# Planned waits of layer 0's attention steps, and the transposes of P and of the convolution in one PSUM bank

## The chip, the cores and the metric

One core of a Trainium2 chip runs the whole program. TensorE (PE) multiplies matrices into PSUM, VectorE (DVE), ScalarE (ACT) and GpSimd (POOL) do elementwise work, and SyncE (SP), ACT and POOL start DMAs. Each engine takes its instructions in the order in which they stand in its own stream and waits on semaphores for the others. The metric is the device time of one execution in microseconds (us); lower is better.

## The reference

A decoder trunk of two layers over 512 tokens of width 1024, in float32. Only the mixer of layer 0 is touched here: attention over a window of 128 tokens (8 query heads, 2 key heads, a learned sink per head) beside a convolution module, with one input and one output projection.

```
def even_mixer(h, w_in, sinks, conv_w, conv_b, ln_g, ln_b, w_out, pos):
    proj = einsum('bsd,de->bse', h, w_in)
    q, k, v, glu = split(proj, [512, 640, 768])
    a = band_attention(rotary(q), rotary(k), v, 127, sinks)      # 8 heads of 64
    g_a, g_b = split(glu, 2)
    c = causal_depthwise_conv(g_a * sigmoid(g_b), conv_w, conv_b)  # 31 taps, 512 channels
    c = silu(layer_norm(c, ln_g, ln_b))
    return einsum('bse,ed->bsd', concatenate([a, c]), w_out)
# trunk: h += mixer(rms_norm(h)); h += swiglu(rms_norm(h)); twice; then rms_norm
```

## The kernel before, in words

Activations lie transposed: 128 features on the partitions, 512 tokens along the row. Every weight block of 128x128 is split into a high and a low part (`w_hi` by ScalarE, `w_lo` by VectorE or, in this mixer, by GpSimd), and a product is three matmuls of 512 columns, L201 to L203 in `acc3`, "a tile" below. A projection onto 128 outputs is 8 tiles, 24 matmuls.

Layer 0's mixer is one list of steps (`C0["steps"]`, L39): `g0` to `g3` are the two projections of a block of the gated unit and its convolution, `k`, `v` and `q0` to `q3` the projections of attention, `S0` to `S3` start the scores of two heads, `V0` to `V3` their product with V, `L` the norm behind the convolution. `A`, `X` and `Y` are tiles of the output projection that read attention's four results, `B` and `C` those that read the convolution's four.

The order of TensorE's stream is written by a small planner at build time, `Seq` (L208). It has a clock, `seq.t`, in estimated microseconds of TensorE work; each tile moves it on by a constant (L204, L265). Scores, values and norms are generators in lines of their own. Each yields a cost and a wait: the planner emits the next piece at the first tile at which the wait is over. So a wait is a number of tiles put between two pieces, and no instruction that waits. Where the next step needs a result, `seq.until` moves the clock on at once to the time of the next piece (L236): no tile is left to put in between. The other engines' streams are ordered by the scheduling layer, which plays the program through a timeline of its own.

The pieces that the change touches:

- `scores0(i)` (L573): waits `q`; 8 score matmuls for the first two blocks of 128 tokens, a wait `S`, 8 for the other two (L590, L591). VectorE takes mask and minimum out of banks 2 and 3 (L598), ScalarE the exponentials into `Pm` (L610), VectorE the sums and `rl` (L605, L614, L615). After a wait `ST` the values may follow.
- `values0(i)` and `pt_av` (L620, L395): P is transposed in four groups into a bank (L407), copied by ScalarE into `pts` (L410) and multiplied with V (L421). `TA` is planned between the transpose and its product, `AO` before the output step: VectorE scales by `rl` into `on` (L430), TensorE transposes `on` (L435), and two engines split it into `oh` and `ol`. Transposes take banks 4 and 7 in turn.
- `conv_tile(j)` (L467): 31 taps of the convolution of 128 channels, the first ones on ScalarE and GpSimd (L478, L479), the others on VectorE, one instruction a tap, accumulating in bank 6 (L481, L483), and a sum into `yc` (L484). They have the lowest priority, so that the scheduling layer puts them between the rest.
- `conv_norm` (L633): for each of the four blocks, not before `ln[j]` on the planner's clock, four transposes of `yc` into bank 7 (L641), statistics (L643), and a copy into `yn` (L644). After the fourth: mean and variance (L650, L652), a power on GpSimd (L654), L656, and `yn` scaled for four token blocks, two on ScalarE (L662) and two on VectorE (L659). After a wait `LB` four groups of transposes back (L668), SiLU (L671) and a split into `oh` and `ol` (L363, L364, L673, L674).

Of the kernel before, what the change touches and what calls it, by code (L numbers as in the profile page):

```python
# [10 lines left out]
def _warn_once_fixed(msg, *args, **kwargs):  # L11
# [13 lines left out]
S = 512  # L25
# [9 lines left out]
C0 = dict(  # L35

    first='a0 b0',  # L39
    steps='L g0 v q0 g1 k S0 q1 S1 V0 g2 q2 q3 S2 V1 g3 S3 V2 V3 A1 A0 A2 Y5 X1 A3 Y6 X3 X0 X2 Y7 B0 B3 C12',  # L40
    na=(0, 1), nx=(2, 3, 4),
    rope_v=('k', 'q2', 'q3'),
    taps=(8, 15, 15, 10),

    norm=(0.0, 2.6), q=5.99, v=0.5, S=3.13, ST=0.86, TA=0.65, AO=1.09, LB=4.85, LO=2.1, ln=(54.8, 69.91, 96.75, 112.86),

    n1=5, q1=6.6, S1=2.26, ST1=3.65, m1=11.78, M1=0.53, TA1=1.12, AO1=1.4,
)
# [86 lines left out]
def trunk_kernel(ctx: ExitStack, tc: tile.TileContext, xT, ws, cols, sinks, sgu_g, sgu_b,  # L135
# [11 lines left out]
    def bank(i, shape=None):  # L147
        return psum.tile(shape or [P, S], F32, name=f"bank{i}")
# [49 lines left out]
    def acc3(ps, x, start, stop):  # L198
        hi, lo = next_tile()
        xh, xl = x  # L200
        T.matmul(ps, hi, xh, start=start, stop=False)  # L201
        T.matmul(ps, hi, xl, start=False, stop=False)  # L202
        T.matmul(ps, lo, xh, start=False, stop=stop)  # L203
        seq.tick(0.648)  # L204

# [35 lines left out]
    seq = Seq()  # L243
# [7 lines left out]
    def tok_gemm(x, banks, each=None, hold=0, ready=None):  # L251

        ps = [bank(b) for b in banks]
        last = len(x) - 1

        def mac(t, k, row):
            hi, lo = row
            xh, xl = x[k]  # L260
            c = slice(t * P, (t + 1) * P)
            T.matmul(ps[t], xh[:, c], hi, start=(k == 0), stop=False)  # L262
            T.matmul(ps[t], xh[:, c], lo, start=False, stop=False)  # L263
            T.matmul(ps[t], xl[:, c], hi, start=False, stop=(k == last))  # L264
            seq.tick(0.648)  # L265

        for k in range(len(x) - hold):
            row = next_row()
            for t in range(NQ):
                mac(t, k, row)  # L270
            if each:
                each(k)
        if hold:
            rows = {k: next_row() for k in range(len(x) - hold, len(x))}
            for t in range(NQ):
                for k, row in rows.items():
                    mac(t, k, row)
                ready(t, ps[t])
        return ps
# [34 lines left out]
    norm = {}  # L314
# [80 lines left out]
    def pt_av(items, vap, rl, dst, banks, line="V", ta="TA", ao="AO"):  # L395

        po = bank(5, [P, 8, 64])
        turn = [0]

        def tbank():  # L400
            turn[0] += 1
            return bank(banks[turn[0] % len(banks)])

        def trans(grp):
            pt = tbank()
            for x, (u, pap, blk, first, last) in enumerate(grp):
                T.transpose(pt[:, x * P:(x + 1) * P], pap, ident)  # L407
            pts = mpool[0].tile([P, S], F32, name="pts", bufs=3)
            w = len(grp) * P
            A.activation(pts[:, :w], pt[:, :w], AF.Copy)  # L410
            return pts

        grps = [items[c:c + 4] for c in range(0, len(items), 4)]
        pts, at = {}, {}
        for g in range(min(2, len(grps))):
            pts[g] = trans(grps[g])
            at[g] = seq.t + 0.43 + C0[ta]
            yield 0.43, (0.0 if g == 0 else max(0.0, at[0] - seq.t - 0.43))
        for g, grp in enumerate(grps):
            for x, (u, pap, blk, first, last) in enumerate(grp):  # L420
                T.matmul(po[:, u, :], pts[g][:, x * P:(x + 1) * P], vap(u, blk), start=first, stop=last)  # L421
            cost = 0.43
            if g + 2 < len(grps):
                pts[g + 2] = trans(grps[g + 2])
                at[g + 2] = seq.t + 0.86 + C0[ta]
                cost = 0.86
            if g + 1 < len(grps):
                yield cost, max(0.0, at[g + 1] - seq.t - cost)
        on = mpool[0].tile([P, NQ, P], F32, name="on", bufs=1)
        V.tensor_mul(on.rearrange("p n (b e) -> p (n b) e", b=2), po,  # L430
                     rl[:, :, None].to_broadcast([P, 8, 64]))
        yield 0.43, C0[ao]
        pt = tbank()
        for n in range(NQ):
            T.transpose(pt[:, n * P:(n + 1) * P], on[:, n, :], ident)  # L435
        split(pt, oh_[0][dst], ol_[0][dst])
        done.add((line, dst))
        yield 0.43, 0.0
# [5 lines left out]
    with ExitStack() as mx:  # L444
# [126 lines left out]
        oh_[0], ol_[0] = oh, ol  # L571

        def scores0(i):  # L573
            yield 0.0, C0["q"]
            while i >= 2 and ("V", i - 2) not in done:
                yield 0.0, 0.3
            qss = qTs[i][1]
            Pm = mp.tile([P, 8, 2 * P], F32, name="Pm", bufs=2)
            nm = scr.tile([P, 8], F32, name="nm")
            l = scr.tile([P, 8], F32, name="l")  # L580
            for n2 in range(2):
                sb = [bank(2), bank(3)]
                for n1 in range(2):
                    n = 2 * n2 + n1
                    for b in range(2):
                        lo = max(n - 1, 0) * P
                        w = (n + 1) * P - lo
                        out = sb[b][:, n1 * 256 + 256 - w:n1 * 256 + 256]
                        q = slice(n * P, (n + 1) * P)
                        T.matmul(out, qss[b][:, q], khh[b][:, lo:lo + w], start=True, stop=False)  # L590
                        T.matmul(out, qss[b][:, q], kl[b][:, lo:lo + w], start=False, stop=True)  # L591
                for n1 in range(2):
                    n = 2 * n2 + n1
                    for b in range(2):
                        u = 2 * n + b
                        c0 = P if n == 0 else 0
                        hd = i + 4 * b
                        V.tensor_tensor_reduce(  # L598
                            out=Pm[:, u, c0:], in0=sb[b][:, n1 * 256 + c0:n1 * 256 + 256],
                            in1=mask0[:, c0:], scale=-0.125, scalar=nsink[:, hd:hd + 1],  # L600
                            op0=ALU.add, op1=ALU.min, accum_out=nm[:, u:u + 1])
                if n2 == 0:
                    yield 0.9, C0["S"]
            es = scr.tile([P, 8], F32, name="es")
            V.tensor_tensor(out=es.rearrange("p (n b) -> p n b", b=2),  # L605
                            in0=nm.rearrange("p (n b) -> p n b", b=2),
                            in1=sinkb[:, i:i + 5:4][:, None, :].to_broadcast([P, NQ, 2]), op=ALU.add)
            for u in range(8):
                c0 = P if u < 2 else 0
                A.activation(Pm[:, u, c0:], Pm[:, u, c0:], AF.Exp, bias=nm[:, u:u + 1], scale=-1.0,  # L610
                             accum_out=l[:, u:u + 1])
            A.activation(es, es, AF.Exp)
            rl = scr.tile([P, 8], F32, name="rl")
            V.tensor_add(rl, l, es)  # L614
            V.reciprocal(rl, rl)  # L615
            del qTs[i]
            pend[i] = Pm, rl, seq.t + 0.9 + C0["ST"]
            yield 0.9, 0.0

        def values0(i):  # L620
            while i not in pend:
                yield 0.0, 0.3
            Pm, rl, at = pend.pop(i)
            yield 0.0, max(0.0, at - seq.t)
            items = []
            for u in range(8):
                n, b = divmod(u, 2)
                if n:
                    items.append((u, Pm[:, u, 0:P], n - 1, True, False))
                items.append((u, Pm[:, u, P:], n, n == 0, True))  # L630
            yield from pt_av(items, lambda u, blk: Vt[:, blk, 64 * (u % 2):64 * (u % 2) + 64], rl, i, (4, 7))

        def conv_norm():  # L633

# [1 line left out]
            bs = scr.tile([P, NQ, 4, 6], F32, name="bs")  # L636
            for j in range(4):
                yield 0.0, max(0.0, C0["ln"][j] - seq.t)
                pt = bank(7)
                for t in range(NQ):  # L640
                    T.transpose(pt[:, t * P:(t + 1) * P], yc[j][:, t * P:(t + 1) * P], ident)  # L641
                for t in range(NQ):
                    V.bn_stats(bs[:, t, j, :], pt[:, t * P:(t + 1) * P])  # L643
                A.activation(y[:, :, j * P:(j + 1) * P], pt.rearrange("p (t c) -> p t c", t=NQ), AF.Copy)  # L644
                yield 0.43, 0.0
# [32 lines left out]
                yield 0.43, (C0["LO"] if 0 < j < 3 else 0.0)  # L678

        qTs, pend, po, ks, early = {}, {}, {}, {}, {}  # L680
        for step in C0["steps"].split():
            kind, i = step[0], int(step[1:] or 0)
            if kind == "g":
# [658 lines left out]
```

## Time and profile before

| | us |
|---|---|
| three runs | 1114.96, 1115.18, 1112.4 |
| their median | 1114.96 |
| the profiled execution | 1111.7 |
| its span, first to last instruction | 1110.0 |
| TensorE busy | 1069.4 (96%) |
| VectorE busy | 694.0 (63%) |
| ScalarE busy | 571.6 (51%) |
| GpSimd busy | 233.2 (21%) |

The profile's shares are over the whole span. Layer 0's mixer lies in the first 190 us of it. A row of a timeline gives the start of an instruction, how long it took, and in brackets how long its engine had been idle before it and which instruction ended that.

### The profile page before, as it was taken

The page shows a single profiled execution, that of the slowest core. Times are in us where ns is not written, and L with a number is a line of the kernel's source. Part 1 is how long each engine was busy: PE and PEld are TensorE (multiplying, and loading weights), DVE is VectorE, ACT ScalarE, POOL GpSimd, SP SyncE. Part 2 cuts the span into 40 slices and gives each one's busy share as a digit, 9 for nine tenths or more (in the row PEclk, how much of TensorE's full clock was granted, in tenths as well). Part 3 has the DMA queues.
Part 4 walks back from the last instruction along what each step waited for, and adds up shares of the span by engine and source line. Part 5 has one row for each costly group of instructions (what it writes and reads, how often), then busy time and mean ns, then how long its engine had stood idle before and what let it go on. Part 6 is the DMA issues. An engine that isn't in the chain of part 4 may idle for free.

```text
span 1110.0 us, 13707 instructions
## 1 busy us (share of the span) xinstructions
PE 1069.4 (96%) x5118; PEld 886.8 (80%) x5118; DVE 694.0 (63%) x1059; ACT 571.6 (51%) x930; POOL 233.2 (21%) x210
## 2 busy tenths in 40 slices
PE   9988889999999999999999999999899999999997
PEld 7767777878888888888887888888788888888785
DVE  3899965876565655564748646666765646555543
ACT  6577756754445353543637654446544443535433
POOL 0799744211101010100024200002110110101002
PEclk9999899999999999999999999999999999999999
DMA  6221112987757676621522112239877676766112
GB/s 228 68 76 58 39 38 76 285 210 192 181 160 169 181 150 198 144 47 57 160 98 83 41 43 72 77 106 269 207 194 188 154 172 185 140 197 143 29 67 76
DMA packets 42803, 145.89 MB, mean 131 GB/s; under 512 B 4848, under 2 KB 5744, under 8 KB 42736
## 3 DMA queue, kind: packets, MB, share of 16 engines
q1 hardware_dynamic: 30496, 100.88, 26.4%
q0 software_dynamic: 11520, 41.95, 22.3%
q10 hardware_dynamic: 720, 2.18, 0.6%
q8 instruction: 40, 0.66, 0.2%
q14 instruction: 27, 0.22, 0.1%
HBM read 142.89 MB, written 2.10 MB: 131 GB/s over the span
## 4 chain that ended last, share of the span: by engine, by line
PE 77%; DVE 10%; DMA 4%; ACT 4%; issue 3%; POOL 2%; POOLq 0%; ACTq 0%; DVEq 0%
PE bank L201 11%; PE bank L202 10%; PE bank L907 10%; PE bank L203 10%; PE bank L908 10%; PE bank L905 10%; DMA raw<-in_ws 4%; PE bank L262 2%; PE bank L264 2%; PE bank L263 2%; DVE bank L483 2%; PE bank L421 2%; PE bank L920 1%; DVE w2l L151 1%; ACT w2h L881 1%
## 5 line engine op out<-in xcount | busy, mean ns | idle before, releaser
L151 DVE TENSOR_TENSOR w2l<-raw,w2h 128x1024 fp32r<-128x1024 f32 x140 | 171.2, 1225 | 204.8 <-ACT w2h L881 200.5
L881 ACT ACTIVATE w2h<-raw 128x1024 fp32r<-128x1024 f32 x140 | 147.8, 1059 | 210.8 <-PE bank L908 159.0
L174 ACT ACTIVATE w_hi<-raw 128x512 fp32r<-128x512 f32 x204 | 127.7, 628 | 178.3 <-PE bank L202 141.2
L871 POOL DMA_DIRECT2D raw<-in_ws x80 | 69.6, 876 | 551.6 <-DVE w2l L151 229.7
L151 DVE TENSOR_TENSOR w_lo<-raw,w_hi 128x512 fp32r<-128x512 f32 x164 | 115.9, 710 | 57.1 <-ACT w_hi L174 57.0
L907 PE MATMUL bank<-w2l,s 128*128 128x512 f32 x320 | 125.0, 391 | 2.7 <-DVE w2l L151 2.7
L905 PE MATMUL bank<-w2h,s 128*128 128x512 f32 x320 | 125.6, 393 | 1.5 <-DVE gb L841 1.3
L908 PE MATMUL bank<-w2h,s 128*128 128x512 f32 x320 | 124.7, 390 | 0.0
L201 PE MATMUL bank<-xh,w_hi 128*128 128x512 f32 x272 | 110.0, 404 | 1.1 <-ACT w_hi L174 1.1
L203 PE MATMUL bank<-xh,w_lo 128*128 128x512 f32 x272 | 106.8, 393 | 0.0
L202 PE MATMUL bank<-xl,w_hi 128*128 128x512 f32 x272 | 106.7, 392 | 0.0
L201 PE MATMUL bank<-hh,w_hi 128*128 128x512 f32 x256 | 99.8, 390 | 0.0
L202 PE MATMUL bank<-hl,w_hi 128*128 128x512 f32 x256 | 99.7, 390 | 0.0
L203 PE MATMUL bank<-hh,w_lo 128*128 128x512 f32 x256 | 99.7, 389 | 0.0
L905 PE MATMUL bank<-w2h,xh 128*128 128x512 f32 x240 | 94.4, 393 | 0.0
L908 PE MATMUL bank<-w2h,xl 128*128 128x512 f32 x240 | 93.5, 390 | 0.0
L907 PE MATMUL bank<-w2l,xh 128*128 128x512 f32 x240 | 93.4, 389 | 0.0
L907 PEld LDWEIGHTS bank<-w2l,s 128*128 128x128 f32 x320 | 60.1, 188 | 16.3 <-DVE w2l L151 4.1
L905 PEld LDWEIGHTS bank<-w2h,s 128*128 128x128 f32 x320 | 60.1, 188 | 15.0 <-DVE gb L841 1.7
L908 PEld LDWEIGHTS bank<-w2h,s 128*128 128x128 f32 x320 | 60.1, 188 | 12.5
L151 POOL TENSOR_TENSOR w_lo<-raw,w_hi 128x512 fp32r<-128x512 f32 x40 | 54.8, 1371 | 58.5 <-ACT w_hi L174 56.0
L479 POOL TENSOR_TENSOR yc<-yc,prod 128x512 f32<-128x512 f32 x44 | 60.6, 1377 | 10.9 <-ACT prod L478 9.5
(237 smaller groups left out, 2056.1 us busy)
## 6 DMA issues: line engine op xcount, KB each, us to landing
raw<-in_ws SPq DMA_DIRECT2D x177, 512.0 KB, 4.3
raw<-in_ws POOLq DMA_DIRECT2D x80, 512.0 KB, 5.7
h<-in_xT SPq DMA_DIRECT2D x8, 256.0 KB, 5.6
raw<-in_ws ACTq DMA_DIRECT2D x4, 512.0 KB, 5.1
out_y<-xh SPq DMA_DIRECT2D x4, 256.0 KB, 2.0
out_y<-xl SPq DMA_DIRECT2D x4, 256.0 KB, 2.3
raw<-in_ws SPq DMA_DIRECT2D x2, 256.0 KB, 4.0
ropeC<-in_rope_c SPq DMA_DIRECT2D x2, 256.0 KB, 4.1
```

Source lines behind the costliest of these rows:

```text
L151: eng.tensor_tensor(out=out, in0=a, in1=b, op=ALU.subtract)
L174: A.activation(hi, src, AF.Copy)
L201: T.matmul(ps, hi, xh, start=start, stop=False)
L202: T.matmul(ps, hi, xl, start=False, stop=False)
L203: T.matmul(ps, lo, xh, start=False, stop=stop)
L262: T.matmul(ps[t], xh[:, c], hi, start=(k == 0), stop=False)
L479: G.tensor_add(yc[j], yc[j], p)
L871: nc.gpsimd.dma_start(t, ws[base + 8 * (g - 1) + 2 * BLOCK_OF[more] + q], accum_op=ALU.add)
L881: A.activation(hi, src, AF.Copy)
L905: T.matmul(ps[t], xh[:, c], wh[:, w], start=(start and j == 0), stop=False, skip_group_check=True)
L907: T.matmul(ps[t], xh[:, c], wl[:, w], start=False, stop=False, skip_group_check=True)
L908: T.matmul(ps[t], xl[:, c], wh[:, w], start=False, stop=(j == 3), skip_group_check=True)
```

## The change

New numbers for the planner; a longer estimate of a tile; the first transposed group goes to bank 4 in place of 7; and two guards: the convolution's transposes are not emitted while a `values0` is under way (`busy`), and no `values0` begins for `LS` = 3.5 after them (`quiet`). No arithmetic is changed. Lines behind L622 move down by 3 to 8 (L641 becomes L648, L643 L650, L668 L675, L717 L725).

```
-    norm=(0.0, 2.6), q=5.99, v=0.5, S=3.13, ST=0.86, TA=0.65, AO=1.09, LB=4.85, LO=2.1, ln=(54.8, 69.91, 96.75, 112.86),
+    norm=(0.0, 2.6), q=(8.5, 6.0, 6.0, 6.0), v=1.2, S=3.13, ST=3.0, TA=0.9, AO=2.4, LB=4.85, LO=2.1, LS=3.5, ln=(60.0, 82.0, 114.0, 135.0),
...
         T.matmul(ps, lo, xh, start=False, stop=stop)
-        seq.tick(0.648)
+        seq.tick(0.682)
...
-            return bank(banks[turn[0] % len(banks)])
+            return bank(banks[(turn[0] - 1) % len(banks)])
...
         def scores0(i):
-            yield 0.0, C0["q"]
+            yield 0.0, C0["q"][i]
...
             yield 0.0, max(0.0, at - seq.t)
+            while seq.t < quiet[0]:
+                yield 0.0, 0.3
+            busy.append(i)
...
             yield from pt_av(items, lambda u, blk: Vt[:, blk, 64 * (u % 2):64 * (u % 2) + 64], rl, i, (4, 7))
+            busy.remove(i)
...
                 yield 0.0, max(0.0, C0["ln"][j] - seq.t)
+                while busy:
+                    yield 0.0, 0.3
+                quiet[0] = seq.t + C0["LS"]
                 pt = bank(7)
```

On TensorE, at the second `values0`, the stream of before has the convolution's second block (`yc_137`, into bank 7) three tiles ahead of the first two groups of P (the rows left out are eight of the nine matmuls of these tiles).

```order
L641 MATMUL bank_1080<-ident,yc_137 128x128 x4
...
L203 MATMUL bank_1109<-xh_143,w_lo 128x512
L407 MATMUL bank_1120<-ident,Pm 128x128 x4
L407 MATMUL bank_1127<-ident,Pm 128x128 x4
```

The changed stream has that block behind the output step of the same values.

```order
L203 MATMUL bank_1099<-xh_143,w_lo 128x512
L407 MATMUL bank_1110<-ident,Pm 128x128 x4
L407 MATMUL bank_1117<-ident,Pm 128x128 x4
...
L435 MATMUL bank_1188<-ident,on 128x128 x4
L201 MATMUL bank_1099<-xh_257,w_hi 128x512
L202 MATMUL bank_1099<-xl_258,w_hi 128x512
L203 MATMUL bank_1099<-xh_257,w_lo 128x512
L648 MATMUL bank_1198<-ident,yc_137 128x128 x4
```

The first and third block move in the same way: from inside the first `values0` to behind it, and from between the halves of the fourth scores to one tile behind the last output step.

On VectorE, at the last output step (`on`, L430), before: the taps of the fourth block (`bank_1280`) and its sum `yc_139` stand ahead of it.

```order
L605 TENSOR_TENSOR es<-nm,sinkb 128x8
L483 SCALAR_TENSOR_TENSOR bank_1280<-cp_127,cc,bank_1280 128x512 x2
L614 TENSOR_TENSOR rl<-l,es 128x8
L483 SCALAR_TENSOR_TENSOR bank_1280<-cp_127,cc,bank_1280 128x512
L615 RECIPROCAL rl<-rl 128x8
L483 SCALAR_TENSOR_TENSOR bank_1280<-cp_127,cc,bank_1280 128x512
L484 TENSOR_TENSOR yc_139<-yc_139,bank_1280 128x512
L430 TENSOR_TENSOR on<-bank_1466,rl 128x512
L364 TENSOR_TENSOR ol_323<-bank_1509,oh_315 128x512
```

After: five of those taps, the sum and four statistics of the third block stand behind it.

```order
L483 SCALAR_TENSOR_TENSOR bank_1280<-cp_127,cc,bank_1280 128x512 x5
L430 TENSOR_TENSOR on<-bank_1456,rl 128x512
L483 SCALAR_TENSOR_TENSOR bank_1280<-cp_127,cc,bank_1280 128x512 x3
L364 TENSOR_TENSOR ol_323<-bank_1499,oh_315 128x512
L483 SCALAR_TENSOR_TENSOR bank_1280<-cp_127,cc,bank_1280 128x512
L650 BN_STATS bs<-bank_1510 128x6 x4
L483 SCALAR_TENSOR_TENSOR bank_1280<-cp_127,cc,bank_1280 128x512
L484 TENSOR_TENSOR yc_139<-yc_139,bank_1280 128x512
L650 BN_STATS bs<-bank_1636 128x6 x4
```

On TensorE, at the end of the mixer, the stream of before has the fourth block of the convolution in the middle of a `Y` step, 24 tile matmuls between it and the first transposes back (L668), and 21 between these and the first tile that reads a result of the convolution (`oh_316`).

```order
L641 MATMUL bank_1572<-ident,yc_139 128x128 x4
...
L203 MATMUL bank_1545<-oh_312,w_lo 128x512
L668 MATMUL bank_1635<-ident,yn 128x128 x4
L668 MATMUL bank_1645<-ident,yn 128x128 x4
...
L203 MATMUL bank_1664<-oh_315,w_lo 128x512
L201 MATMUL bank_1331<-oh_316,w_hi 128x512
...
L668 MATMUL bank_1702<-ident,yn 128x128 x4
```

After, the fourth block stands behind the last tile of attention's results; nothing stands between it, the first transposes back and the first tile of the convolution, nor between the last transposes back and the tile that reads their result (`oh_319`; 12 tile matmuls lay there before).

```order
L203 MATMUL bank_1617<-oh_315,w_lo 128x512
L648 MATMUL bank_1636<-ident,yc_139 128x128 x4
L675 MATMUL bank_1663<-ident,yn 128x128 x4
L675 MATMUL bank_1673<-ident,yn 128x128 x4
L201 MATMUL bank_1331<-oh_316,w_hi 128x512
...
L675 MATMUL bank_1701<-ident,yn 128x128 x4
...
L203 MATMUL bank_1545<-oh_316,w_lo 128x512
L675 MATMUL bank_1718<-ident,yn 128x128 x4
L201 MATMUL bank_1331<-oh_319,w_hi 128x512
```

## Rows read from the trace of the kernel before

**Rows 1.** Whom TensorE waited for, 30 to 190 us: total, times, longest.

```profile
PE bank L435 <- DVE on L430: 4.0, 3, 1.9
PE bank L407 <- ACT yn L644: 3.8, 2, 2.8
PE bank L591 <- DVE kl L698: 3.8, 2, 2.5
PE bank L421 <- ACT pts L410: 2.1, 3, 1.3
PE bank L565 <- DVE ga L704: 1.1, 1, 1.1
```

**Rows 2.** Busy time by stretch: PE, PEld, DVE, ACT, POOL; granted clock; DMA.

```profile
73.90:115.20 41.30, 35.73 (x207) 30.32 (x206) 40.91 (x81) 32.32 (x72) 35.64 (x27) 0.96 0.16 52
115.20:138.00 22.80, 19.45 (x105) 16.95 (x106) 21.24 (x42) 16.48 (x38) 18.20 (x15) 0.89 0.13 47
152.50:180.80 28.30, 28.17 (x132) 22.68 (x133) 9.96 (x19) 15.09 (x23) 16.41 (x13) 1.00 0.24 75
```

**Rows 3.** The chain of waits, 20 to 190 us: start, duration, what.

```profile
73.91 0.69 DVE ga L501
...
115.21 0.70 DVE on L430
```

**Rows 4.** Timeline of VectorE where it was idle for TensorE.

```profile
73.91 0.69 DVE L501 TENSOR_TENSOR ga<-bank,R 128x512 f32<-128x512 f32 x1 [1.40 <-PE bank L203]
...
138.08 0.69 DVE L430 TENSOR_TENSOR on<-bank,rl 128x512 f32<-128x512 f32 x1 [0.80 <-PE bank L421]
```

**Rows 5.** VectorE by line, 68.9 to 152 us: count, busy us, mean ns.

```profile
L483 DVE SCALAR_TENSOR_TENSOR bank<-cp,cc,bank 128x512 f32<-128x512 f32 x49 | 36.7, 749 | 0.6
L605 DVE TENSOR_TENSOR es<-nm,sinkb 128x8 f32<-128x8 f32 x4 | 3.5, 884 | 0.0
L643 DVE BATCH_NORM_STATS2 bs<-bank 128x6 f32<-128x128 f32 x12 | 2.6, 281 | 0.0
L484 DVE TENSOR_TENSOR yc<-yc,bank 128x512 f32<-128x512 f32 x3 | 2.0, 680 | 0.1
```

**Rows 6.** Timeline of TensorE behind the last output step.

```profile
152.54 0.66 PE L435 MATMUL bank<-ident,on 128*128 128x128 f32 x4 [1.24 <-DVE on L430]
...
160.61 0.60 PE L641 MATMUL bank<-ident,yc 128*128 128x128 f32 x4
160.96 0.48 PE L201 MATMUL bank<-oh,w_hi 128*128 128x512 f32 x1
...
173.85 0.60 PE L668 MATMUL bank<-ident,yn 128*128 128x128 f32 x4
...
177.50 0.51 PE L202 MATMUL bank<-yc,w_hi 128*128 128x512 f32 x1
```

**Rows 7.** Timeline of ScalarE in the norm behind the convolution.

```profile
165.37 1.52 ACT L662 ACTIVATE yn<-yn,nmr,rs 128x512 f32<-128x512 f32 x2 [1.59 <-DVE nmr L656]
...
167.43 1.28 ACT L671 ACT_TABLE_LOAD   x1
168.72 1.45 ACT L671 ACTIVATE ga<-bank,cc 128x512 f32<-128x512 f32 x2
170.06 0.63 ACT L363 ACTIVATE oh<-ga 128x512 fp32r<-128x512 f32 x1
```

**Rows 8.** The same stretch on VectorE, and a short instruction ahead of it.

```profile
147.84 0.16 DVE L605 TENSOR_TENSOR es<-nm,sinkb 128x8 f32<-128x8 f32 x1
...
165.38 1.87 DVE L659 TENSOR_SCALAR yn<-yn,rs,nmr 128x512 f32<-128x512 f32 x2
170.20 0.43 DVE L673 CAST oh<-ga 128x512 fp32r<-128x512 f32 x1 [2.96 <-ACT ga L671]
...
171.28 0.68 DVE L364 TENSOR_TENSOR yc<-ga,oh 128x512 fp32r<-128x512 f32 x1
...
175.30 1.42 DVE L673 CAST oh<-ga 128x512 fp32r<-128x512 f32 x1 [1.62 <-ACT ga L671]
```

More of the change, by code (lines that the diff above doesn't have):

```diff
@@ L264, in mac @@
             T.matmul(ps[t], xl[:, c], hi, start=False, stop=(k == last))
-            seq.tick(0.648)
+            seq.tick(0.682)
         for k in range(len(x) - hold):
@@ L680, in trunk_kernel @@
         qTs, pend, po, ks, early = {}, {}, {}, {}, {}
+        busy, quiet = [], [0.0]
         for step in C0["steps"].split():
```

## The prediction

> **What bounds the kernel now.** I read the waits of TensorE first. Over the whole span it is busy 96%, so a wait in layer 0's mixer is time lost once, and nothing behind it gives it back. In the mixer the largest sums are waits for the output step's scaling (4.0 us in 3 times), for the copy out of bank 7 that stands between the convolution's transposes and those of P (3.8), for the low part of k (3.8), and for copies of P (2.1) [rows 1]. The change addresses all of these except that for k, so read by itself this view promises some ten microseconds.
>
> The second view is busy time by stretch. From 73.9 to 115.2 us VectorE is busy 40.91 of 41.30 us, TensorE 35.73; from 115.2 to 138, 21.24 and 19.45 of 22.80 [rows 2]. The third is the chain of waits: between its rows at 73.91 and at 115.21 every longer piece is VectorE's, the second being the scaling of the second output step [rows 3]. So in the attention part VectorE, which has all the convolution's taps beside its share of the softmax, sets the pace, and TensorE's waits are where it runs into VectorE. A wait taken out of TensorE's plan there comes back at the next output step, unless VectorE has less to do before it.
>
> The fourth is the stretch behind the last output step, 152.5 to 180.8: TensorE is busy 28.17 of 28.30 us at a granted clock of 1.00 [rows 2], which is the higher of its two levels, 2.4 GHz. No wait is to be won there, and one can be lost.
>
> **Part 1: what the attention part can gain.** I measure it at the last output step, whose transposes start at 152.54 [rows 6].
>
> First, the scale for the norm comes one tile (three matmuls, 0.7) earlier and the transposes of v one tile later, so the 1.1 us for which these waited goes [rows 1], and VectorE gets its first inputs 0.7 to 1.1 earlier. VectorE's chain starts 0.8 earlier: gain 0.8.
>
> Second, VectorE does less before the last output step. Five taps at 0.749, the sum at 0.680 and four statistics at 0.22 (2.6 for 12) now stand behind it [rows 5]: 3.7 + 0.7 + 0.9 = 5.3. Behind it they are hidden: the block that needs them is transposed some 17 us later, behind 75 tile matmuls.
>
> Third, VectorE's idle time. 1.40 at 73.91 was a wait for the projection a2; more of it now stands ahead of the first scores, so this goes. The 0.80 at 138.08 was a wait for products with V [rows 4]. At that place ScalarE's stream now has the tanh of the last gated unit ahead of the first copy of P, and the start of the fourth convolution block ahead of the third copy, so this wait stays, and with it TensorE's wait for copies of P. Gain 1.4.
>
> Sum 7.5: the last output step starts at about 145.0. All other planned waits (`q`, `ST`, `TA`, `AO`, and the freed bank 7) I cost at nothing beyond this: the stalls they remove come back as waits for `on`, since tiles put ahead of an output step do not make VectorE reach it sooner. The ends: 3, if VectorE gains no idle time and its long instructions fall worse, and 11, if it loses no time at all and the 0.80 goes too.
>
> **Part 2: what the end of the mixer loses.** `ln[3]` goes from 112.86 to 135.0 while a tile grows only from 0.648 to 0.682. So the fourth block's transposes come behind the last tile that needs attention alone; then the planner moves its clock on, and `LB` and `LO` have no tiles left to put in between.
>
> The norm. Before, from the start of those transposes at 160.61 [rows 6] to the end of the last scaled piece at 165.38 + 1.87 = 167.25 [rows 8] are 6.64 us, covered by 24 matmuls and more. Now TensorE has only the four transposes (160.96 - 160.61 = 0.35 [rows 6]) and, at the end, three of the next four, 0.3: idle 6.0.
>
> SiLU. The second scaling on ScalarE ends 165.37 + 1.52 = 166.89, 6.28 behind the start. The table load of 1.28, SiLU of 0.73 (1.45 for two) and the high part of 0.63 follow [rows 7], so the first `oh` is there at 8.9. TensorE has done both groups of transposes by 7.1 (6.64 and two times 0.35, less the 0.3): idle 1.8; 21 matmuls covered it before. The second matmul of the tile needs the low part, 0.68 on VectorE [rows 8], of which the first matmul covers 0.23: idle 0.45.
>
> The load shows 1.28 and SiLU starts 0.01 behind its end [rows 7]. The Trainium skill, page "ScalarE: Activation LUTs", section "What ACT_TABLE_LOAD costs", gives about 1.28 us for the load and a drain of about 1.38 beside it. By that the wait here would be 1.4 longer and the sum 1.4 higher; the row has no room for a drain, and I go by the row.
>
> The last group. Before, from its transposes at 173.85 to the matmul that reads the low part at 177.50 are 3.65 us [rows 6], with a cast that took 1.42 where another took 0.43 [rows 8]. TensorE now has 0.35 and 0.23 to do in it, so idle between 2.1 and 3.1. I take 2.2, near the short cast, since GpSimd has less to do then. 12 matmuls covered it before, but for 0.2.
>
> The third block's transposes move behind the last output step: 0.35. Sum: 6.0 + 1.8 + 0.45 + 2.2 - 0.2 + 0.35 = 10.6.
>
> The clock. The granted clock was 0.96 over 41.3 us and 0.89 over 22.8 [rows 2], stretches with waits of TensorE of 1 to 3 us in them. At the lower level (half) that is 41.3 x 0.04 = 1.7 and 22.8 x 0.11 = 2.5 us of work lost in each. The end of the mixer, at 1.00 before, now gets two such places, behind the wait for the last output step and behind the norm. What is lost inside a wait costs nothing, so I take 1.5 each: 3.0, with the ends 0 and 5.
>
> So part 2 costs 13.6, between 10.5 and 16.
>
> **Sum.** 13.6 - 7.5 = 6.1 us slower. The profiled execution took 1111.7 (span 1110.0 and 1.7 around it): 1117.8. The median of the runs before, 1114.96, is 3.3 above that execution, so against the runs the forecast is 1121.
>
> **The rivals.**
>
> TensorE is the bound, and the stalls go as planned. All of [rows 1] but 2.3 of the wait for k is 12.5; with the lower clock in the two stretches (4.2) that is 16.7 gained, less 13.6: 3.1 faster, 1112. For it: the waits are there, and each named one has tiles put into it. Against it: VectorE's 40.91 of 41.30. It decides from a gain of 13.6 on. With still more gain in smaller waits it would be 1108.
>
> VectorE's work itself gets shorter. The instruction for `es`, of 8 columns, took 0.884 in the mean of four and 0.16 at its shortest [rows 5, 8]; long ones come while GpSimd is at work, so where the two streams meet decides. The Trainium skill, page "SBUF — State Buffer", section "Who interferes with whom", says that a VectorE instruction with two SBUF inputs and a GpSimd instruction that reads SBUF shut each other out; the trace agrees, by those two numbers. The streams meet otherwise now. If all four of these fell to the shortest, 2.9 would go; with as much from the other two-input instructions, 5.8, and the sum falls to about 0: 1115. The same mechanism can add as much: 1127.
>
> The clock stays up. Without the 3.0, and with the 0.80 at 138.08 gone as well, the sum is +2.3: 1117, within the spread of a measurement.
>
> The end is worse. Waits of 6.0, 1.8 and 2.2 in a row keep the clock down for all that follows them up to the last `C` tile (5), and the gain ahead of it is only 3, since the third values wait longer behind the fourth block's work on ScalarE: 10.6 + 5 - 3 = 12.6, 1127 to 1128.
>
> **How the numbers follow.** A measurement of this kernel tells about 0.3%, 3.3 us, from no change. The forecast, slower by 3.3 to 10: 0.48. The end worse: 0.13. No difference that can be told, by shorter work of VectorE or by a clock that stays up: 0.28. TensorE the bound, or VectorE's time shrinking further: faster, 0.11. So faster 0.11, same 0.28, slower 0.61. The range leaves out half of the worst case and most of the faster one: 1113 to 1127; the forecast's own range is 1118.5 to 1125.
>
> **What would show it.** Right: no wait for the copy into `yn` at L407; waits for `on` that stay at three or four us in sum or grow, with VectorE as dense as before up to the last output step; that step near 145; then, behind the fourth block's transposes, a wait of TensorE of about 6 us for `yn`, one near 2 for `oh` behind SiLU and one near 2 at the first tile of the last block; a granted clock under 1.00 behind them. Wrong in part 1: the last output step before 141 or behind 150. Wrong in part 2: no wait at L675 over 3 us. The forecast falls if the time is below 1115 although those waits are there: then TensorE was held by its plan and not by VectorE.

## The result and the profile after

The changed kernel took 1120.83 us (median of 4 runs, 1119.0 to 1122.99), the kernel before 1114.94 (4 runs beside them). The ratio is 1.0058, 95% interval 1.004 to 1.0076: slower by 6.5 us (4.5 to 8.5). The profiled execution took 1121.24, its span 1119.5.

The waits of TensorE after, 30 to 190 us (whom it waited for: total, times, longest), against [rows 1]:

```profile
PE bank L675 <- ACT yn L669: 4.9, 1, 4.9
PE bank L421 <- ACT pts L410: 4.8, 3, 1.9
PE bank L201 <- DVE gb L498: 3.0, 1, 3.0
PE bank L201 <- ACT oh L363: 2.4, 2, 1.2
PE bank L591 <- DVE kl L706: 2.1, 1, 2.1
PE bank L407 <- ACT Pm L610: 1.6, 1, 1.6
PE bank L201 <- DVE oh L680: 1.5, 1, 1.5
PE bank L435 <- DVE on L430: 1.4, 2, 0.8
```

The 3.8 us for the copy out of bank 7 are gone, those for `on` fell from 4.0 to 1.4, those for the low part of k (`kl`) from 3.8 to 2.1, and those for v (`ga`) are gone. New are the first, fourth (half of it) and seventh row, all at the end of the mixer, and more waiting for `pts` (2.1 before), `gb` and `Pm`. The last two stood like this before:

```profile
PE bank L201 <- DVE gb L498: 1.3, 1, 1.3
PE bank L407 <- ACT Pm L610: 0.2, 1, 0.2
```

Busy time by stretch (PE, PEld, DVE, ACT, POOL; granted clock; DMA), cut at the transposes of the second, third and last output step, of the fourth block, and at the first `C` tile, against [rows 2]:

```profile
88.80:110.40 21.60, 19.40 (x118) 16.50 (x116) 20.25 (x37) 15.13 (x33) 19.65 (x14) 1.00 0.15 50
110.40:132.80 22.40, 19.15 (x108) 16.21 (x109) 21.46 (x45) 17.69 (x41) 18.45 (x15) 0.92 0.15 48
132.80:149.40 16.60, 12.51 (x63) 10.73 (x61) 14.20 (x35) 9.09 (x27) 8.68 (x7) 0.71 0.00 0
149.40:170.00 20.60, 20.60 (x86) 16.97 (x87) 5.48 (x11) 5.96 (x10) 10.32 (x8) 0.91 0.23 77
170.00:191.60 21.60, 13.69 (x51) 9.92 (x50) 7.32 (x18) 9.93 (x14) 5.40 (x5) 0.76 0.08 24
```

VectorE is still the densest engine up to 132.8. In the third row nobody is dense: VectorE is 2.4 us idle, TensorE 4 us and at a clock of 0.71. The last two rows are the end of the mixer; before, all of it ran at 1.00 with hardly a wait. TensorE there, against [rows 6] (start, duration, in brackets the idle time ahead):

```profile
170.01 0.60 PE L648 MATMUL bank<-ident,yc 128*128 128x128 f32 x4
175.53 2.25 PE L675 MATMUL bank<-ident,yn 128*128 128x128 f32 x8 [4.92 <-ACT yn L669]
178.99 0.80 PE L201 MATMUL bank<-oh,w_hi 128*128 128x512 f32 x1 [1.21 <-ACT oh L363]
179.71 0.80 PE L202 MATMUL bank<-yc,w_hi 128*128 128x512 f32 x1
...
180.73 0.63 PE L201 MATMUL bank<-oh,w_hi 128*128 128x512 f32 x1
181.16 0.63 PE L202 MATMUL bank<-yc,w_hi 128*128 128x512 f32 x1
...
184.32 0.60 PE L675 MATMUL bank<-ident,yn 128*128 128x128 f32 x4
...
185.46 0.60 PE L675 MATMUL bank<-ident,yn 128*128 128x128 f32 x4
187.58 0.49 PE L201 MATMUL bank<-oh,w_hi 128*128 128x512 f32 x1 [1.53 <-DVE oh L680]
188.31 0.50 PE L202 MATMUL bank<-yc,w_hi 128*128 128x512 f32 x1 [0.23 <-DVE yc L681]
...
191.41 0.39 PE L203 MATMUL bank<-oh,w_lo 128*128 128x512 f32 x1
191.64 0.39 PE L201 MATMUL bank<-oh,w_hi 128*128 128x512 f32 x1
```

The matmuls at 180.73 and 181.16 start 0.43 apart, those at 191.41 and 191.64 0.23: the lower and the higher level of the clock. What TensorE waited for at 175.53 and 178.99, on ScalarE, against [rows 7]:

```profile
174.66 1.52 ACT L669 ACTIVATE yn<-yn,nmr,rs 128x512 f32<-128x512 f32 x2 [2.49 <-DVE nmr L663]
176.20 1.28 ACT L678 ACT_TABLE_LOAD   x1
177.50 0.78 ACT L678 ACTIVATE ga<-bank,cc 128x512 f32<-128x512 f32 x1
178.30 0.63 ACT L363 ACTIVATE oh<-ga 128x512 fp32r<-128x512 f32 x1
```

The last output step starts at 149.37 (152.54 before), the first `C` tile at 191.64 (180.84). Between them lie 42.3 us in place of 28.3. Behind it the profiled execution took 929.6 us, 1.3 less than before (930.9). So in this pair of executions the change costs 14.0 - 3.2 - 1.3 = 9.5 us, 3 more than in the runs.

### The profile page after: what moved, and what is told of

The parts are those of the page before. It is cut to its first block, busy times and chain, and to the rows that moved or that the text cites. A ratio compares the mean times of both kernels' runs of the same rounds, so it can differ in the third digit from the quotient of the medians.

```text
span 1119.5 us, 13712 instructions
## 1 busy us (share of the span) xinstructions
PE 1073.8 (96%) x5118; PEld 891.2 (80%) x5118; DVE 694.6 (62%) x1059; ACT 571.1 (51%) x930; POOL 234.2 (21%) x210
## 4 chain that ended last, share of the span: by engine, by line
PE 78%; DVE 10%; DMA 5%; ACT 4%; issue 2%; POOL 1%; POOLq 0%; ACTq 0%; DVEq 0%
PE bank L201 11%; PE bank L202 11%; PE bank L203 10%; PE bank L916 10%; PE bank L915 10%; PE bank L913 10%; DMA raw<-in_ws 5%; PE bank L262 2%; PE bank L264 2%; PE bank L263 2%; PE bank L421 2%; DVE bank L483 2%; PE bank L928 1%; DVE w2l L151 1%; PE bank L407 1%
## 5 line engine op out<-in xcount | busy, mean ns | idle before, releaser
L151 DVE TENSOR_TENSOR w2l<-raw,w2h 128x1024 fp32r<-128x1024 f32 x140 | 171.2, 1225 | 204.9 <-ACT w2h L889 204.7
L151 DVE TENSOR_TENSOR w_lo<-raw,w_hi 128x512 fp32r<-128x512 f32 x164 | 117.7, 721 | 57.6 <-ACT w_hi L174 55.5
L151 POOL TENSOR_TENSOR w_lo<-raw,w_hi 128x512 fp32r<-128x512 f32 x40 | 56.1, 1405 | 70.6 <-ACT w_hi L174 59.8
```

The source lines that it names most:

```text
L151: eng.tensor_tensor(out=out, in0=a, in1=b, op=ALU.subtract)
```

## The experiments

All ratios are to the kernel before, run beside. For every profile I cut the mixer at three places: the first mask reduction (L598), the transposes of the last output step (L435), and the first `C` tile. Behind that the profiled executions took between 928.4 and 936.5 us, so a single time says less than the columns.

The kernels do differ a little behind the mixer, contrary to what stands above on layer 0 alone: layer 1 uses the tile estimate too, and with 0.682 four pieces of its attention stand one tile away from their old place. Counted along TensorE's stream, the stretch with all four (580 to 700 us in the kernel before) took 120.0, 121.5 and 121.5 us in the three kernels with 0.648, and 119.2 to 122.1 in the eight with 0.682: what this is worth is lost in the spread.

| kernel | ratio (95%) | first reduction at | from it to last step | from there to C |
|---|---|---|---|---|
| before | | 68.96 | 83.6 | 28.3 |
| changed | 1.0058 (1.004 to 1.0076) | 67.75 | 81.6 | 42.3 |
| block 4 early | 0.9983 (0.9967 to 0.9999) | 71.77 | 79.5 | 31.1 |
| before, block 4 late | 1.0101 (1.0084 to 1.0118) | 69.05 | 85.0 | 39.9 |
| tail filled | 1.0066 (1.0048 to 1.0083) | 69.24 | 78.3 | 41.4 |
| bank 1 first | 1.0066 (1.0042 to 1.0091) | 73.35 | 78.1 | 40.5 |
| q0 on GpSimd | 0.9984 (0.9969 to 1.0) | 67.60 | 81.6 | 31.2 |
| 8 taps less, third block | one run, 1107.35 | 71.78 | 74.9 | 29.3 |
| 14 taps less, fourth block | one run, 1112.18 | 69.38 | 77.0 | 29.3 |
| guards only | 1.0009 (0.9992 to 1.0025) | 69.04 | 86.5 | 30.4 |
| numbers only | 1.0032 (1.001 to 1.0055) | 69.40 | 89.1 | 31.2 |

**The changed kernel with the fourth block early.**

```
-    ... ln=(60.0, 82.0, 114.0, 135.0),
+    ... ln=(60.0, 82.0, 114.0, 120.0),
```

> The changed kernel with one number altered: ln[3] = 120 in place of 135, so that the fourth block's transposes stand 8 tiles behind the last output step, with 8 tiles between them and the first transposes back and 10 more ahead of the first tile that reads a result of the convolution. Theory T (the loss is the end of the mixer, where the norm and SiLU stand bare; the attention part is a gain): no wait of TensorE over 1 us behind the last output step, 28 to 30 us from its transposes to the first C tile (42.3 in the changed kernel, 28.3 before), last output step still near 149.4; time 1107 to 1111, below the kernel before by 0.3 to 0.7%. Rival R (the loss comes from the attention part: the guards, the longer planned waits and the 3.0 us wait at the first A tile, and the end only shows it): the time stays above 1116.

Measured 1112.71 (12 runs, 1108.8 to 1115.96), 0.17% under the kernel before, just clear of no change, and 8.4 us (0.75%) under the changed one by the ratios. The waits behind the last output step shrank to 0.39 and 0.27 at L675. So the loss is the end of the mixer, and the rest of the change is a small gain: theory T. The sizes missed: the time is 1.7 above the upper end of what I expected, the last output step stood at 151.31 and not near 149.4, and the end took 31.1 and not 28 to 30. In this profile the front took 4 us more (below); whether that holds for the median of the runs isn't shown.

**The kernel before with the fourth block late.**

```
-    ... ln=(54.8, 69.91, 96.75, 112.86),
+    ... ln=(54.8, 69.91, 96.75, 131.0),
```

> The kernel before with one number altered: ln[3] = 131 in place of 112.86; nothing else of the change. The fourth block's transposes then stand behind the last tile of attention's results, as in the changed kernel. Theory T: TensorE waits some 5 us for yn and 1 to 2 each for oh twice, the stretch from the last output step to the first C tile grows by 12 to 14; VectorE has the four statistics of that block later but all taps as before, so the last output step stays within 1 us of 152.5; time 1125 to 1130. Rival R: within 4 of the kernel before, 1111 to 1119.

1125.45, slower by 11.3 us (9.4 to 13.2), with these waits:

```profile
PE bank L435 <- DVE on L430: 7.0, 4, 3.4
PE bank L668 <- ACT yn L662: 4.9, 1, 4.9
...
PE bank L201 <- ACT oh L363: 1.8, 2, 1.2
PE bank L201 <- DVE oh L673: 1.5, 1, 1.5
```

One number, `ln[3]`, alone costs more than the whole change lost. In this profile the end took 39.9, 11.6 more than before (12 to 14 expected), and the last output step came at 154.03, 1.5 later than before (1 expected at most).

**The end of the mixer filled with matmuls.**

```
+            fill(20)          # behind the fourth block's transposes
...
+                if kind == "B":
+                    fill({0: 11, 3: 8}[i])
```

> The changed kernel with extra matmuls of 128x512 into bank 5, which nobody reads, in the places where TensorE waits at the end of the mixer: 20 behind the fourth block's transposes, 11 ahead of the first B tile, 8 ahead of the last block's first tile (39 in all, 8.9 us at 0.2275 each). They add work and take no wait away. Theory T (of the 14.0 us lost there some 8 are waits and 4 to 6 are work at the lower clock behind them): granted clock 0.95 or more from 170 to 190 in place of 0.74 to 0.83, the tile matmuls behind the first wait at 0.23 in place of 0.43, first C tile 2 to 4 us earlier; time 1117 to 1119. Rival C (the half pace there doesn't come from the waits, or the lost clock lies under the waits and costs nothing): within 1 us of the changed kernel, or slower by up to 3.

The clock did what theory T said, by the windows ahead of and behind the fourth block's transposes:

```profile
147.50:168.10 20.60, 20.57 (x86) 16.85 (x87) 5.54 (x11) 5.96 (x10) 10.29 (x8) 0.92 0.24 77
168.10:189.00 20.90, 19.30 (x91) 14.90 (x90) 7.29 (x18) 9.83 (x14) 5.53 (x5) 1.00 0.08 26
```

The time did not: 1.0066, not faster than the changed kernel's 1.0058, and the stretch to `C` shrank by only 0.8 (41.4 against 42.3). By the time this is rival C. The rows say why, and they don't say that the clock was worth nothing:

```profile
168.14 0.60 PE L653 MATMUL bank<-ident,yc 128*128 128x128 f32 x4
178.96 0.50 PE L202 MATMUL bank<-yc,w_hi 128*128 128x512 f32 x1 [0.78 <-DVE yc L364]
182.73 0.60 PE L681 MATMUL bank<-ident,yn 128*128 128x128 f32 x4
```

```profile
175.66 1.45 ACT L684 ACTIVATE ga<-bank,cc 128x512 f32<-128x512 f32 x2
177.00 0.63 ACT L363 ACTIVATE oh<-ga 128x512 fp32r<-128x512 f32 x1
```

From the matmul that reads the first low part to the last transposes back it is 3.77 us (178.96 to 182.73) where the changed kernel takes 5.75 (179.71 to 185.46): the higher clock gave back 2.0. But from the fourth block's transposes to that matmul it is 10.8 (from 168.14) where the changed kernel takes 9.7 (from 170.01). Here ScalarE's stream has both SiLUs ahead of the first `oh`, and TensorE waits 0.78 for a low part that it did not wait for before; that lost 1.1. So it isn't a clean test of what the clock costs. The 8.9 us of extra matmuls themselves lie in waits.

**Bank 1 ahead of bank 0 in A1** (the two weight blocks of this step don't change places with the banks, so this kernel adds wrong products to two sums; its times are used alone).

```
+                if step == "A1":
+                    ns = ns[::-1]
```

> The changed kernel with the two tiles of A1 in the other order, bank 1 ahead of bank 0. Bank 1's projection is read at 116.4 by VectorE, bank 0's at 122.3, and the wait of 3.0 us at 123.11 is for the latter. Theory T1 (between the third and the last output step TensorE's chain, at a granted clock of 0.73, lost the gain of the attention part, and this wait is what lowered the clock ahead of it): the wait falls to about 1 (for Pm), the granted clock from 131 to 149 rises above 0.85, the last output step comes 1.5 to 4 us earlier, and so does the end: 1117 to 1119.5. Rival V (VectorE and ScalarE set the third output step, and the clock there falls for its own later waits): the wait moves to the transposes of P or to the products, last output step within 1 us of 149.4, time within 1.5 of the changed kernel.

The wait for `gb` fell from 3.0 to 1.3, that for `pts` rose from 4.8 to 5.3, and the time stayed (1.0066, seven runs from 1115.32 to 1126.21). The clock between the third and the last output step was 0.79, under the 0.85 of theory T1. The wait moved on: rival V, though a gain of 2 us would not be seen in runs spread this far. The stretch from the first reduction to the last step is 3.5 shorter here, but three profiles whose streams are the same up to there on every engine (changed, block 4 early, tail filled) lie nearly as far apart, from 78.3 to 81.6. Here the stretch from the last output step to the fourth block's transposes ran at the higher clock:

```profile
151.49 0.66 PE L435 MATMUL bank<-ident,on 128*128 128x128 f32 x4 [0.93 <-DVE on L430]
...
170.32 0.60 PE L648 MATMUL bank<-ident,yc 128*128 128x128 f32 x4
```

**q0's low part on GpSimd.** In the front of the first experiment VectorE and GpSimd show this (timelines of the two engines):

```profile
50.24 5.67 DVE L725 TENSOR_TENSOR qs<-qT,qs 64x512 fp32r<-64x512 f32 x1
```

```profile
50.33 1.30 POOL L479 TENSOR_TENSOR yc<-yc,prod 128x512 f32<-128x512 f32 x1
51.57 2.55 POOL L151 TENSOR_TENSOR w_lo<-raw,w_hi 128x512 fp32r<-128x512 f32 x2
54.07 1.30 POOL L479 TENSOR_TENSOR yc<-yc,prod 128x512 f32<-128x512 f32 x1
59.56 1.27 POOL L479 TENSOR_TENSOR yc<-yc,prod 128x512 f32<-128x512 f32 x1 [4.19 <-ACT prod L478]
```

In the changed kernel, with the same streams up to there, VectorE's instruction took 0.70, and GpSimd's first one 1.77 in place of 1.30:

```profile
50.24 0.70 DVE L725 TENSOR_TENSOR qs<-qT,qs 64x512 fp32r<-64x512 f32 x1
```

```profile
50.33 1.77 POOL L479 TENSOR_TENSOR yc<-yc,prod 128x512 f32<-128x512 f32 x1
```

The four GpSimd instructions in a row are two additions and two low parts of weights (L151), not four additions.

```
-                        V.tensor_tensor(out=qss[b][rows[1 - b]], ...
+                        (G if i == 0 else V).tensor_tensor(out=qss[b][rows[1 - b]], ...
```

> The kernel of the first experiment (block 4 early) with the low part of q0 (L725, two instructions of 64x512) computed by GpSimd in place of VectorE. In two of four profiles of kernels whose streams are the same up to there, the first of them took 5.67 and 5.70 us while GpSimd had four additions in a row (50.3 to 55.4), in the other two 0.70. Theory P (which of the two engines gets in first differs from run to run, and this one instruction moves everything behind it by 4 us): no VectorE instruction over 2 us ahead of 70, first mask reduction at 67 to 69, the same in every run, last output step at 146 to 149; time 1108 to 1111, its runs no more than 4 apart (1108.8 to 1115.96 in the first experiment). Rival Q (the front is set by the weights or by ScalarE; VectorE catches up in waits it has anyway): first reduction still at 70 or later, time within 1 of 1112.7.

The front came out as said, 67.60 and no long instruction, but the time is that of the first experiment (0.9984), and the runs spread as far (1111.36 to 1118.13). From the first to the second output step TensorE now took 26.3 us where it took 21.1. Theory P is right on the instruction and wrong on its worth and on the spread.

**Fewer taps: 8 of the third block, 14 of the fourth** (left out of the convolution).

```
-                for t in range(TAPS):
+                for t in range(23 if j == 2 else TAPS):      # third block
+                for t in range(17 if j == 3 else TAPS):      # fourth block, the other kernel
```

> The kernel of the first experiment without the last 8 of 31 taps of the convolution's third block: 8 instructions of VectorE at 0.75, 6.0 us, which stand between the second and the third output step, are left out. If VectorE sets the pace there, as the prediction has it, the third output step comes 4 to 6 us nearer to the second (22.4 to 22.9 us between their transposes with all taps); if TensorE or ScalarE does, less than 1.5.

> The kernel of the first experiment without the last 14 of 31 taps of the convolution's fourth block, 10.5 us of VectorE, of which 6 taps stood behind the last output step and 8 or more ahead of it, between the third and the last. If VectorE sets the pace there, as the prediction has it, the last output step comes 4 to 6 us nearer to the third (16.6 us between their transposes in the changed kernel and in the first experiment, 13.3 in the kernel before). Theory: there the chain of the last values (scores, exponentials, transposes, copies, products) is the longer one, and the stretch stays within 1.5 of 14.5 to 16.6, nearer to 14.5 if the granted clock is high.

Third block: from the second to the third output step 20.1 in place of 22.7 us, 2.7 of the 6.0 taken out; neither expectation. VectorE sets the pace there until 2.7 us are gone; then it waits 2.5 for GpSimd's part of the convolution, and the products with V end at 131.23, 0.03 ahead of `on`. Fourth block: from the third to the last step 12.8, with the clock at 1.00, and VectorE waits for TensorE:

```profile
145.63 0.69 DVE L430 TENSOR_TENSOR on<-bank,rl 128x512 f32<-128x512 f32 x1 [2.17 <-PE bank L421]
```

That is below the 14.5 to 16.6 that I set for the theory, and 3.8 below the first experiment, just short of the 4 to 6 of the other reading; part of the 3.8 is the clock, 1.00 where it was 0.71. Both kernels leave arithmetic out and ran once, so only their stretches are used.

**The guards and the bank order alone.** (All of `C0`'s numbers and 0.648 as before; `q` four times 5.99, `LS` = 3.5.)

> The changed code (both guards and the order of the banks) with all numbers of the kernel before (waits, tile estimate, ln). The two waits for the copy out of bank 7, 3.8 us in the kernel before, go. Theory (they come back as waits for VectorE at the output steps): last output step within 1.5 of 152.5, time 1113 to 1116. Rival (TensorE was held by its plan): last output step 2 to 4 earlier, time 1110 to 1112.

1.0009, no gain, but neither reading was tested: the waits that were to go did not. The one for `yn` at L407 stayed at 3.0 in two times, so the guard of 3.5 doesn't do its work with the old `ln`, and the last output step came later than either had it, at 155.5.

**The numbers alone** (`ln[3]` = 120).

```
-            while seq.t < quiet[0]: ...
-            busy.append(i)
-                while busy: ...
-                quiet[0] = seq.t + C0["LS"]
-            return bank(banks[(turn[0] - 1) % len(banks)])
+            return bank(banks[turn[0] % len(banks)])
```

> The kernel of the first experiment (all new numbers, ln[3] = 120) without the two guards and with the old order of the banks. With the guards and the bank order alone the time was 1.0009 of the kernel before, with numbers and guards 0.9983. Theory (the planned waits and the later blocks bring the gain, since they change how many taps VectorE has ahead of each output step; the guards bring nothing): first mask reduction to last output step 77 to 81 us (83 to 84 before), time 0.996 to 1.000 of the kernel before. Rival G (the guards are what makes the numbers pay): waits for the copy out of bank 7 of 3 us or more come back in sum and the time is 1.001 to 1.004.

1.0032: rival G. The second output step, into bank 7, stands behind a convolution block in that bank:

```profile
113.93 0.60 PE L641 MATMUL bank<-ident,yc 128*128 128x128 f32 x4
121.97 1.12 PE L435 MATMUL bank<-ident,on 128*128 128x128 f32 x4 [7.44 <-ACT yn L644]
```

One copy of 0.57 us, but it stands in ScalarE's stream behind the exponentials of the next scores. Which of the three edits (two guards, bank order) prevents this was not tried apart.

## Why the prediction was right or wrong

**The sum** was right: forecast 6.1 slower, measured 6.5 by the ratio and 5.9 between the medians. That it came out to half a microsecond is partly luck. Part 2 was right term by term; part 1 was larger than any profile shows, and the pair of profiled executions alone would have given 9.5.

**Part 2, the end.** The mechanism is shown: the number alone costs 11.3 us, and taking it back brings 8.4 (the ends of the two profiles differ by 11.2). The sizes are in the profile after. From the fourth block's transposes (170.01) to the matmul that reads the first low part (179.71) it is 9.7 us; the forecast's chain of norm, table load, SiLU, high and low part was 8.9 + 0.68 = 9.6. From the last transposes (185.46) to the matmul behind their low part (188.31) it is 2.85; the forecast had 0.35 + 0.23 + 2.2 = 2.8. The waits by name look smaller than forecast (4.9 for 6.0, 1.2 for 1.8, none for 0.45), because transposes and a first tile at half pace stand in the same chain; that cost nothing, as the forecast had it. Outside the chain the lower clock cost its full price in two places, as forecast: 2.0 between the first low part and the last transposes (5.75 against 3.77 in the filled tail), and 1.8 ahead of the fourth block, where the changed kernel takes 20.6 from the last output step at a clock of 0.91 and the bank-1-first kernel, with the same matmuls, 18.8 at 1.00. I had 1.5 each. So the end cost 14.0 in the profile after (forecast 13.6). With block 4 late neither the third block's transposes nor the lower clock ahead of the fourth block are in it; without these the forecast is 13.6 - 0.35 - 1.5 = 11.8, and 11.6 (profile) and 11.3 (runs) were measured. The table load left no room for a drain here either (176.20 + 1.28, SiLU at 177.50).

**Part 1, the attention part.** Forecast 7.5, ends 3 and 11. The last output step came 3.2 earlier in the profile after, at 149.4 and not near 145. In those of block 4 early and bank 1 first it stands at 151.3 and 151.5, behind the 150 that I had set as the sign of being wrong. By the runs the gain is 4.7 in one way (the first experiment, 1.9 faster with 2.8 more at its end) and 7.0 in another (11.3, with the 0.35 and 1.8 that block 4 late lacks, less 6.5), each to some 3 us. So there is a gain, the 7.5 was too large by the profiles, and the runs don't fix its size. Taken apart:

- VectorE's shorter work. From the first reduction to the last step the profiles have 83.6 and 85.0 without the change, and 81.6, 79.5, 78.3, 78.1 and 81.6 with it (the last with q0 on GpSimd): 2.0 to 6.9 less, where I had 5.3 + 1.4. Five taps, the sum and four statistics did go behind the last step, but other taps moved in: between the third and the last step stand 14 taps (10.5 us) where 10 taps, a sum and four statistics (9.1) stood before. Without these 14 the stretch takes 12.8, 1.8 less than the 14.6 of the filled tail.
- The clock, which I had costed at the end alone. In the profile after it took 2.0 of the gain between the third and the last step: 16.6 us at 0.71, where the filled tail, with the same streams up to there, took 14.6 (133 to 147.5) at 0.99.
- "VectorE sets the pace" held only in part: of 6.0 us less in front of the third step 2.7 came through. The waits for `on` did not stay at 4 as I said they would; they fell to 1.4, and `gb`, `pts`, `Pm` and `oh` took their place.
- The front. Forecast 0.8 gained; the first reduction lay between 1.2 earlier and 4.4 later. Some 4 us of this is whether the two engines block each other in one instruction (71.77 against 67.75, from the same start). This is the mechanism of the second rival, with more in one place (5.67 - 0.70 = 5.0) than I had for all four `es` (2.9). The Trainium skill, page "SBUF — State Buffer", section "Who interferes with whom", says that a VectorE instruction with two SBUF inputs contends with a GpSimd instruction that reads SBUF, and that the ports which they share are an exclusive lock. The trace agrees by those two durations; here the loser waited through four instructions of the other, though by its start it was 0.09 ahead of the first of them. Removing it gained nothing in the time.

**Guards and bank 7**, which I cost at nothing: alone they bring nothing (1.0009), but as a part of the change they are worth something. Without them the new numbers lose 0.49% (1.0032 against 0.9983), and in that profile the second output step waits 7.4 us behind a convolution block in its bank. Numbers and guards need each other, and a sum over parts can't show that.

**The rivals.** "TensorE is the bound" is out: it needed 16.7 us gained ahead of the last output step, and 3.2 came. "VectorE's work gets shorter" is out for this profile: its four `es` took 3.1 us in place of 3.5, but its four `rl` 3.5 in place of 2.4. "The clock stays up" is out by 0.71 and 0.76. "The end is worse" was close in the profile (gain 3.2, end 14.0, where it had 3 and 15.6), not in the time.

What stays open: why the clock was 0.71 in one profile and 0.99 in another between the third and the last step with the same waits ahead; and what spreads the runs of one kernel over 7 us: the front's collision isn't it, and the part behind the mixer alone differs by 8 between the profiles. Counted along TensorE's stream, this lies mainly in two places, the first 119 us behind the first `C` tile (117.6 to 123.8) and the 120 us around layer 1's attention (119.2 to 122.1); the cause stays open.

## What to carry to other kernels

A step that waits on a long chain of other engines must start while its own engine still has independent work to put in front of it; one number that moved it behind the last such work cost 11 us here, and the version with that number at 120 is the fastest of the three (0.9983, 0.9967 to 0.9999). Reckon such a chain from the rows at full pace (9.6 forecast, 9.7 measured) and add a clock loss only for the work outside it: slow work inside a wait cost nothing here, the tiles between two waits 2.0. Edits that keep two users of a buffer apart and edits that move these users are to be costed together.

## What the runs showed of the hardware

- One VectorE instruction of 64x512 took 0.70 or 5.67 us from the same start, 50.24; in the second case it ended only behind four GpSimd instructions in a row.
- 39 extra matmuls in waits, 8.9 us of work by estimate (0.2275 each), held the granted clock at 1.00 where it had been 0.76. The tiles between the waits then took 3.8 us in place of 5.7; another order on ScalarE cost 1.1 of that again, and the time showed no gain.
- With one stream the granted clock of a 16 us stretch was 0.71 in one profile and 0.99 in another; the stretch took 2.0 us longer in the first.
